# Zeros below the upper activations: the FFN tail's second product on 128 rows in place of 64

## The chip, the cores and the metric

The kernel runs on one core of one Trainium2 chip. The metric is the device time in microseconds (us) of one execution. A core has TensorE (PE in the profile; its weight loads stand apart as PEld), VectorE (DVE), ScalarE (ACT), GpSimd (POOL) and SyncE (SP, which issues most DMAs). Each engine works through its own instructions in order; semaphores tie the engines together. A product on TensorE is two instructions: a weight load (LDWEIGHTS) of the stationary block and a MATMUL that streams the moving block past it.

## The reference, cut to what matters

The model is a trunk of two layers on 512 tokens of 1024 features in float32. Each layer has an FFN, a token mixer and a second FFN; a last RMSNorm ends it. The FFN is the part that the change touches, and it runs four times:

```python
D_FF = 2752
def swiglu(h, w_gate, w_up, w_down):
    return (jax.nn.silu(h @ w_gate) * (h @ w_up)) @ w_down
x = x + 0.5 * swiglu(rmsnorm(x, ffn1_norm[layer]), ...)
```

2752 is 21 blocks of 128 hidden features and a rest of 64. This rest is the tail.

## The kernel before, in words

Features lie on the 128 partitions (rows), tokens along the free dimension. Every float32 operand of a product is split in an upper part ("hi", a rounded copy) and a lower part ("lo", what the rounding left), and a product of two operands is three matmuls: `whi*xhi`, `wlo*xhi`, `whi*xlo` (`mm3`, L244 to L246). The weight blocks come by DMA as `raw`; ACT makes `whi` (L206) and DVE `wlo` (L212), two units ahead of the products that use them.

An FFN goes in thirds of its hidden features: 8, 7 and then 7 blocks, the last of these being the tail (block 21). For each block there is a gate unit and an up unit of 24 matmuls (`over_x`, into banks `ps_A`). VectorE and ScalarE turn their results into `hhi` and `hlo`. After each third come eight down units, one for each 128 output features (`down`, into banks `ps_mm`): three matmuls for each hidden block, then `x += 0.5*ps` (L475) and the next norm's scaled and split input (L297, L303) and squares.

The tail's gate and up parts, 64 features each, share one unit. Its evacuation is `evac_tail` (L436 to L451), which stands first in the third, some 12 units ahead of the down units. It leaves the activations in a tile `both`: the upper part on rows 0 to 63 and the lower part on rows 64 to 127. The down weights' last block holds the same 64 rows twice. So one 128-row matmul (L470) gives `whi*hhi + whi*hlo`, and a second one on rows 0 to 63 alone (L471) gives `wlo*hhi`:

```python
both = st.h[TAIL][0]
nc.tensor.matmul(ps, u.hi[:, j * 128:(j + 1) * 128], both, start=False, stop=False)
nc.tensor.matmul(ps, u.lo[0:64, j * 128:(j + 1) * 128], both[0:64], start=False, stop=True)
```

A down unit of the last third thus has 20 matmuls: 18, L470 and L471. The next unit starts with a 128-row product again. In the fourth FFN the last third's down units run in two passes, one for each half of the tokens (`last_down`, L540 and L541, 256 columns), so that the final norm can begin early; its factors are broadcast by L583 after the third unit of the second pass.

The order on every engine is the order of emission. Outside the first layer's mixer that is the order of the Python code; in the mixer a planner sets it from fixed estimates, which do not depend on the FFN. During the first FFN, DVE, POOL and PE also work out tables for the mixer between the units (L735 to L954).

Of the kernel before, what the change touches and what calls it, by code (L numbers as in the profile page):

```python
# [46 lines left out]
class Unit:  # L47
    """A stationary weight block [128, cols], the products that use it and what follows them."""

# [9 lines left out]
class Sched:  # L59
    """Orders tasks on the engines by estimated start, then priority, and emits them in that order.  # L60

    A task takes tokens (tile slots) when it starts and gives tokens back when it ends; tokens go to
    the waiting tasks in order of priority, but for the tags in `loose`. A task of `any` engine goes to
    the one of its (engine, duration) pairs that ends first, and gets it as its argument."""

# [73 lines left out]
class Trunk:  # L139
# [6 lines left out]

    # ---------------------------------------------------------------- set-up
    def pools(self):
# [41 lines left out]

    # ---------------------------------------------------------------- weight stream
    def load(self, n):
# [22 lines left out]
    def advance(self):  # L215
        """Splits the next weight block and loads one further ahead."""
        n = self.split
        if n < len(self.units):
            self.cut_hi(n)
            self.cut_lo(n)  # L220
        if n + RAW_BUFS < len(self.units):
            self.load(n + RAW_BUFS)

    def drive(self):
        """Emits the steps in order; weights are loaded and split ahead of their products."""
        self.prologue()
        for s in self.steps:
            if isinstance(s, Unit):
                if s.own is None:
                    self.advance()  # L230
                s.products(s)
                if s.after is not None:
                    s.after()
                if s.own is not None:
                    self.advance()
            else:
                s()

    def mm3(self, ps, pairs, start=True, stop=True):
        """ps += sum over (whi, wlo, xhi, xlo) of the product at float32's accuracy."""  # L240
        nc = self.nc
# [6 lines left out]
    def over_x(self, tag, keep):  # L248
        """Products of one [1024 -> 128] block with the scaled activations."""

# [11 lines left out]
    def over_x_two(self, tag, units, keeps):  # L262
        """The products of two blocks in turns, so that each part of x serves both when it comes."""
        banks = []
# [7 lines left out]

    # ---------------------------------------------------------------- norms
    def feed_norm(self, which, k):
        """Adds tile k of x to the sum of squares and makes its part of x*g, split."""
        self.feed_xg(which, k)
        self.feed_sq(which, k)
# [60 lines left out]
    def norm_mm(self):  # L338
        """Sums over the features, tokens on the partitions."""
        self.nps = self.bank("mm")  # L340
        for t in range(4):
            self.nc.tensor.matmul(
                self.nps[:, t:t + 1], self.acc[:, t * 128:(t + 1) * 128], self.ones[:, 0:1], start=True, stop=True)
# [5 lines left out]
    def norm_pow(self, n=4):  # L349
        """(mean(x^2) + eps)^-1/2."""  # L350
        self.np_ = self.tp.tile([128, 4], F32, tag="np", name="np_", bufs=2)
        self.nc.gpsimd.tensor_tensor(self.np_[:, 0:n], self.nv[:, 0:n], self.mhalf[:, 0:n], ALU.pow)

    def norm_r(self, n=4, at=0):
        """One Newton step."""
        v, p = self.nc.vector, self.np_[:, 0:n]
# [9 lines left out]
    def norm_diag(self, n=4):  # L366
        """r on the diagonal, split."""
        v = self.nc.vector
# [29 lines left out]

    # ---------------------------------------------------------------- SwiGLU
    def ffn(self, n, nxt):  # L400
        """x += 1/2 FFN n; nxt names the norm that follows."""
        st = self
# [34 lines left out]
        def evac_tail(keep):  # L437
            def run():
# [11 lines left out]
                nc.vector.tensor_tensor(both[64:128], s[64:128], hi[64:128].bitcast(F32), ALU.subtract)  # L450
                st.h[TAIL] = (both, None)  # L451
            return run

        def down(dt, third):
# [4 lines left out]
            def products(u):  # L459
# [7 lines left out]
                if TAIL in fs:  # L467
                    j = nf - 1
                    both = st.h[TAIL][0]
                    nc.tensor.matmul(ps, u.hi[:, j * 128:(j + 1) * 128], both, start=False, stop=False)  # L470
                    nc.tensor.matmul(ps, u.lo[0:64, j * 128:(j + 1) * 128], both[0:64], start=False, stop=True)  # L471

# [43 lines left out]
    def last_down(self, units):  # L516
        """The last products and the final norm, one half of the tokens after the other.

        The first half is scaled with its features on the partitions; the second is transposed while
        its norm is worked out."""  # L520
        st, nc = self, self.nc
# [7 lines left out]
        def products(dt, h):  # L529
# [8 lines left out]
            j = len(full)  # L538
            both = st.h[TAIL][0]
            nc.tensor.matmul(p, u.hi[:, j * 128:(j + 1) * 128], both[:, c], start=False, stop=False)  # L540
            nc.tensor.matmul(p, u.lo[0:64, j * 128:(j + 1) * 128], both[0:64, c], start=False, stop=True)  # L541

# [17 lines left out]
        def sums(h, n):  # L560
            """The squares of all features but the last 128, then of these."""
            if n == 0:
# [69 lines left out]

    # ---------------------------------------------------------------- gated short convolution
    def short_conv(self, nxt):
# [71 lines left out]

    # ---------------------------------------------------------------- S5 tables
    def bc(self, ap, shape, axis):
        return ap.unsqueeze(axis).to_broadcast(shape)

    def exp_poly(self, out, x, tmp, itmp):
        """exp of a small tile in float32 by range reduction and a polynomial."""
        nc = self.nc
# [19 lines left out]
    def cmul_parts(self, v, orr, oi, ar, ai, br, bi, t):  # L733
        """(orr + i oi) = (ar + i ai)(br + i bi); the results may not overlay the operands."""
        v.tensor_tensor(orr, ar, br, ALU.mult)  # L735
# [11 lines left out]
    def s5_tables(self):  # L747
        """Works out the S5 tables and leaves them in DRAM by quarter (8 groups), in small pieces."""
        st, nc, a = self, self.nc, self.a
# [208 lines left out]

    # ---------------------------------------------------------------- layer 0: S5 beside stick-breaking attention
    def masks(self):  # L960
        """-[k' >= k], -1, the causal mask's -1e30 and the identity, for float32r products."""
        nc = self.nc
# [21 lines left out]
    def mixer(self, nxt):  # L984
        """Layer 0's token mixer as tasks of the engines."""
        st, nc, a = self, self.nc, self.a
# [29 lines left out]

        # ---- weights
        units = []

        def stream(src, prio):  # L1020
            """A further weight block; its task ends when it is loaded and split."""
            u = Unit(src, 1024, None, None)
            units.append((u, prio))
            return u

        # ---- the units over x
        def over_x(src, prio, tag, gate=None):
# [25 lines left out]

        # ---- v, tokens on the partitions
        vb, vps = [], []
# [37 lines left out]

        # ---- S5
        tab_t, u_t, y_t, h_t = {}, {}, {}, {}
# [118 lines left out]

        # ---- q and k
        qk_t = {}
# [27 lines left out]

        # ---- attention
        c_t, w_t, s_t, scored, split = {}, {}, {}, {}, {}
        ORDER = (1, 3, 2, 0)

        def head(h):
# [99 lines left out]
            def values():  # L1349
                """Rows 0 to 63 gather the products of v's upper part, rows 64 to 127 those of its lower part."""  # L1350
                o = H["o"] = st.bank("mm")
# [34 lines left out]

        # ---- the S5 gate
        add(None, 0, None, [qus[7].last] + [u.last for u in qus], 130.0, rel=["xhi"] * 8 + ["xlo"] * 8)
# [26 lines left out]
        def quarter(u, j, src, deps, prio, rel):  # L1415
            """Products of the j-th [512 -> 128] block of a unit with four split tiles."""
            X = {}
# [56 lines left out]

        # ---- the output projection, S5's half and attention's
        x_t = {}
# [23 lines left out]

        # ---- the weight stream
        units.sort(key=lambda x: x[1])
# [23 lines left out]

    # ---------------------------------------------------------------- ends
    def prologue(self):
# [37 lines left out]
    def warm_up(self):  # L1566
        """Keeps the tensor engine busy, so that its clock is up when the first data comes."""
        t = self.bank("mm")
# [68 lines left out]
def layout(i):  # L1637
    """The inputs as the device reads them: blocks that are contiguous on each partition."""
    import numpy as np
# [60 lines left out]
def result(got):  # L1700
    """The tokens' first half lies with features first, the second with tokens first."""
    import numpy as np
# [18 lines left out]
```

## Time and profile before

| what | value |
| --- | --- |
| median of 3 runs (lowest, highest) | 1892.98 us (1892.46, 1894.23) |
| profiled execution, first to last instruction | 1893.3 us |
| PE busy | 1878.5 us, 99% |
| PEld busy | 1539.3 us, 81% |
| DVE, ACT, POOL busy | 1052.8, 611.2, 130.3 us |
| mean granted TensorE clock | 0.996 of full |

The profiled execution's own time is its span of 1893.3 us; the page gives nothing that lies outside it. The median of the runs is 0.3 us less. Matmuls are pipelined and the profile models their ends, so that a duration (0.39 us) overlaps the next one; what a product costs is read from the distance between two starts.

### The profile page before, as it was taken

What the parts mean: (1) busy time and instruction counts of PE and PEld (TensorE: products, weight loads), DVE (VectorE), ACT (ScalarE), POOL (GpSimd) and SP (SyncE); (2) the same over time, 40 slices, a digit from 0 to 9 for tenths busy, and PEclk for the clock granted to TensorE, in tenths of its full rate; (3) what the DMA queues carried; (4) which work ended last, traced back from release to release, by engine and by line L of the source; (5) the groups of instructions that cost most, each with busy time, mean ns of one, the idle gap of its engine ahead of it and who ended that gap; (6) DMA issues with size and microseconds to landing.
All of it is one profiled execution on the core that took longest, in us unless ns stands there. A gap on an engine that the chain in (4) does not pass through costs nothing.

```text
span 1893.3 us, 21863 instructions
## 1 busy us (share of the span) xinstructions
PE 1878.5 (99%) x8562; PEld 1539.3 (81%) x8562; DVE 1052.8 (56%) x1617; ACT 611.2 (32%) x854; POOL 130.3 (7%) x247
## 2 busy tenths in 40 slices
PE   9999999999999999999999999999999999999998
PEld 7888888788777888888878888887788888888888
DVE  6657777556898553444455434445555554344453
ACT  4312222323764432222232222233322332122233
POOL 0280000100020200000010000000100100000000
PEclk9999999999989999999999999999999999999999
DMA  4334344446211232222222322322222223223231
GB/s 156 118 95 145 111 146 128 130 161 217 79 45 54 72 112 98 100 89 101 94 96 96 96 98 92 98 100 89 101 98 92 95 90 105 100 89 96 96 107 47
DMA packets 76551, 195.63 MB, mean 103 GB/s; under 512 B 20048, under 2 KB 27232, under 8 KB 76448
## 3 DMA queue, kind: packets, MB, share of 16 engines
q1 hardware_dynamic: 76272, 194.20, 31.3%
q8 instruction: 67, 1.10, 0.2%
q14 instruction: 36, 0.29, 0.0%
q10 hardware_dynamic: 144, 0.03, 0.0%
q0 software_dynamic: 32, 0.01, 0.0%
HBM read 180.45 MB, written 12.58 MB: 102 GB/s over the span
## 4 chain that ended last, share of the span: by engine, by line
PE 95%; DVE 2%; DMA 1%; ACT 1%; issue 0%; SPq 0%; POOL 0%; DVEq 0%; POOLq 0%; ACTq 0%
PE ps_A L244 19%; PE ps_A L246 19%; PE ps_A L245 19%; PE ps_mm L244 9%; PE ps_mm L246 9%; PE ps_mm L245 9%; PE ps_A L1037 1%; PE ps_mm L1425 1%; PE ps_A L1039 1%; PE ps_A L1038 1%; PE ps_mm L1426 1%; PE ps_mm L1427 1%; PE ps_A L1323 1%; PE ps_mm L471 1%; PE ps_A L1269 1%
## 5 line engine op out<-in xcount | busy, mean ns | idle before, releaser
L244 PE MATMUL ps_A<-xhi,whi 128*128 128x512 f32 x1568 | 612.9, 391 | 0.8 <-ACT whi L1557 0.8
L245 PE MATMUL ps_A<-xhi,wlo 128*128 128x512 f32 x1568 | 611.2, 390 | 0.5 <-DVE wlo L1558 0.5
L246 PE MATMUL ps_A<-xlo,whi 128*128 128x512 f32 x1568 | 610.9, 390 | 0.0
L212 DVE TENSOR_TENSOR wlo<-raw,whi 128x1024 fp32r<-128x1024 f32 (+1 forms) x322 | 399.0, 1240 | 122.3 <-ACT whi L206 120.7
L206 ACT CAST whi<-raw 128x1024 fp32r<-128x1024 f32 (+1 forms) x324 | 331.4, 1024 | 392.7 <-PE ps_mm L246 232.5
L244 PEld LDWEIGHTS ps_A<-xhi,whi 128*128 128x128 f32 x1568 | 294.8, 188 | 63.7 <-ACT whi L1557 1.4
L245 PEld LDWEIGHTS ps_A<-xhi,wlo 128*128 128x128 f32 x1568 | 294.8, 188 | 62.6 <-DVE wlo L1558 1.1
L246 PEld LDWEIGHTS ps_A<-xlo,whi 128*128 128x128 f32 x1568 | 294.7, 188 | 61.6
L244 PE MATMUL ps_mm<-hhi,whi 128*128 128x512 f32 (+1 forms) x672 | 262.5, 391 | 0.0
L246 PE MATMUL ps_mm<-hlo,whi 128*128 128x512 f32 (+1 forms) x672 | 258.5, 385 | 0.0
L245 PE MATMUL ps_mm<-hhi,wlo 128*128 128x512 f32 (+1 forms) x672 | 257.3, 383 | 0.0
L475 DVE SCALAR_TENSOR_TENSOR x<-ps_mm,x 128x512 f32<-128x512 f32 x88 | 60.8, 691 | 170.6 <-PE ps_mm L246 152.3
L244 PEld LDWEIGHTS ps_mm<-hhi,whi 128*128 128x128 f32 x672 | 126.3, 188 | 30.5 <-issue 5.6
L246 PEld LDWEIGHTS ps_mm<-hlo,whi 128*128 128x128 f32 x672 | 126.2, 188 | 27.5
L245 PEld LDWEIGHTS ps_mm<-hhi,wlo 128*128 128x128 f32 x672 | 126.2, 188 | 25.5
L421 ACT ACTIVATE s<-t 128x512 f32<-128x512 f32 x84 | 53.1, 632 | 290.4 <-DVE t L419 290.4
L432 ACT CAST hhi<-s 128x512 fp32r<-128x512 f32 x84 | 52.2, 621 | 288.7 <-DVE s L431 288.7
L419 DVE TENSOR_TENSOR t<-ps_A,rb 128x512 f32<-128x512 f32 x84 | 57.9, 690 | 110.6 <-PE ps_A L246 104.4
L431 DVE TENSOR_TENSOR s<-ps_A,s 128x512 f32<-128x512 f32 x84 | 58.0, 690 | 108.0 <-PE ps_A L246 107.4
L422 DVE TENSOR_TENSOR s<-s,rb 128x512 f32<-128x512 f32 x84 | 58.3, 694 | 63.3 <-ACT s L421 63.3
L293 POOL TENSOR_TENSOR acc<-acc,sq 128x512 f32<-128x512 f32 x28 | 36.4, 1300 | 827.9 <-issue 623.1
L433 DVE TENSOR_TENSOR hlo<-s,hhi 128x512 fp32r<-128x512 f32 x84 | 58.2, 693 | 57.7 <-ACT hhi L432 57.7
(350 smaller groups left out, 1607.0 us busy)
## 6 DMA issues: line engine op xcount, KB each, us to landing
raw<-gu SPq DMA_DIRECT2D x170, 512.0 KB, 3.3
raw<-dn SPq DMA_DIRECT2D x64, 448.0 KB, 3.3
raw<-dn SPq DMA_DIRECT2D x32, 512.0 KB, 3.5
raw<-sci SPq DMA_DIRECT2D x24, 512.0 KB, 3.2
raw<-ab SPq DMA_DIRECT2D x16, 512.0 KB, 3.3
raw<-abo SPq DMA_DIRECT2D x8, 512.0 KB, 3.3
raw<-sco SPq DMA_DIRECT2D x8, 512.0 KB, 3.2
x<-xT SPq DMA_DIRECT2D x8, 256.0 KB, 5.4
```

What stands on the lines that cost most here:

```text
L206: self.nc.scalar.copy(u.hi[:, : u.cols], u.raw[:, : u.cols])
L212: (engine or self.nc.vector).tensor_tensor(u.lo[:, :c], u.raw[:, :c], u.hi[:, :c].bitcast(F32), ALU.subtract)
L244: nc.tensor.matmul(ps, whi, xhi, start=start and i == 0, stop=False)
L245: nc.tensor.matmul(ps, wlo, xhi, start=False, stop=False)
L246: nc.tensor.matmul(ps, whi, xlo, start=False, stop=stop and i == n - 1)
L419: nc.vector.tensor_tensor(t, pg, st.rb, ALU.mult)
L421: nc.scalar.activation(s, t, AF.Silu)
L422: nc.vector.tensor_tensor(s, s, st.rb, ALU.mult)
L431: nc.vector.tensor_tensor(s, pu, s, ALU.mult)
L432: nc.scalar.copy(hi, s)
L433: nc.vector.tensor_tensor(lo, s, hi.bitcast(F32), ALU.subtract)
L475: nc.vector.scalar_tensor_tensor(x, keep[0], 0.5, x, ALU.mult, ALU.add)
```

## The change

The tail's upper part gets a tile of its own, `hi`, on all 128 rows: the activations on rows 0 to 63 (a third ScalarE copy) and zeros on rows 64 to 127 (a memset on GpSimd, once DVE has read what stood there). The second product then runs on all 128 rows of the lower weights, with this tile as its moving operand. The rest of the diff takes out comments; from L451 on, lines stand two lower in the changed kernel.

```diff
 evac_tail:
                 nc.scalar.copy(hi[64:128], s[64:128])
                 nc.scalar.copy(both[0:64], s[64:128])
                 nc.vector.tensor_tensor(both[64:128], s[64:128], hi[64:128].bitcast(F32), ALU.subtract)
-                st.h[TAIL] = (both, None)
+                nc.scalar.copy(hi[0:64], s[64:128])
+                nc.gpsimd.memset(hi[64:128].bitcast(F32), 0.0)
+                st.h[TAIL] = (both, hi)
 down:
-                    both = st.h[TAIL][0]
+                    both, upper = st.h[TAIL]
                     nc.tensor.matmul(ps, u.hi[:, j * 128:(j + 1) * 128], both, start=False, stop=False)
-                    nc.tensor.matmul(ps, u.lo[0:64, j * 128:(j + 1) * 128], both[0:64], start=False, stop=True)
+                    nc.tensor.matmul(ps, u.lo[:, j * 128:(j + 1) * 128], upper, start=False, stop=True)
 last_down:
-            both = st.h[TAIL][0]
+            both, upper = st.h[TAIL]
             nc.tensor.matmul(p, u.hi[:, j * 128:(j + 1) * 128], both[:, c], start=False, stop=False)
-            nc.tensor.matmul(p, u.lo[0:64, j * 128:(j + 1) * 128], both[0:64, c], start=False, stop=True)
+            nc.tensor.matmul(p, u.lo[:, j * 128:(j + 1) * 128], upper[:, c], start=False, stop=True)
```

On PE no instruction is added or moved. This is the end of a down unit of the first FFN's last third and the start of the next, before and then after (`hi_2427` is the new tile).

```order
L246 MATMUL ps_mm<-hlo,whi 128x512
L470 MATMUL ps_mm<-both,whi 128x512
L471 MATMUL ps_mm<-both,wlo 128x512
L244 MATMUL ps_mm<-hhi,whi 128x512
L245 MATMUL ps_mm<-hhi,wlo 128x512
```

```order
L246 MATMUL ps_mm<-hlo,whi 128x512
L472 MATMUL ps_mm<-both,whi 128x512
L473 MATMUL ps_mm<-hi_2427,wlo 128x512
L244 MATMUL ps_mm<-hhi,whi 128x512
L245 MATMUL ps_mm<-hhi,wlo 128x512
```

The second product keeps its place and takes another moving tile. (The shape in these rows is that of the result.)

On POOL the memset comes in among the table memsets of the first FFN. The first fence is before, the second after; `np_` is the norm's power, `acc` the sum of squares.

```order
L906 MEMSET qco 128x8
L907 MEMSET qsi 128x8
L906 MEMSET qco 128x8
L907 MEMSET qsi 128x8
L293 TENSOR_TENSOR acc<-acc,sq 128x512 x7
```

```order
L908 MEMSET qco 128x8
L909 MEMSET qsi 128x8
L452 MEMSET hi_2427 64x512
L908 MEMSET qco 128x8
L909 MEMSET qsi 128x8
L293 TENSOR_TENSOR acc<-acc,sq 128x512 x7
```

The zeros stand behind the third pair of table memsets and ahead of the fourth. In each of the other three FFNs the memset stands between the norm's power and the next work of POOL. On ACT the third copy stands right behind the second one, once for each FFN.

## Rows read from the trace of the kernel before

**Rows 1.** The profile page: busy time, share and instructions of each engine.

```profile
PE 1878.5 (99%) x8562; PEld 1539.3 (81%) x8562; DVE 1052.8 (56%) x1617; ACT 611.2 (32%) x854; POOL 130.3 (7%) x247
```

**Rows 2.** The profile page: shares of the chain of waits that ended last.

```profile
PE 95%; DVE 2%; DMA 1%; ACT 1%; issue 0%; SPq 0%; POOL 0%; DVEq 0%; POOLq 0%; ACTq 0%
```

**Rows 3.** Timeline of FFN 1's first tail: start, duration, engine, line, shapes, [idle before].

```profile
347.25 0.39 PE L245 MATMUL ps_mm<-hhi,wlo 128*128 128x512 f32 x1
...
348.87 0.39 PE L246 MATMUL ps_mm<-hlo,whi 128*128 128x512 f32 x1
348.87 0.19 PEld L470 LDWEIGHTS ps_mm<-both,whi 128*128 128x128 f32 x1
349.10 0.39 PE L470 MATMUL ps_mm<-both,whi 128*128 128x512 f32 x1
349.42 0.18 PEld L471 LDWEIGHTS ps_mm<-both,wlo 64*128 64x128 f32 x1 [0.36 <-issue]
...
349.85 0.19 PEld L244 LDWEIGHTS ps_mm<-hhi,whi 128*128 128x128 f32 x1 [0.25 <-issue]
...
350.19 0.39 PE L245 MATMUL ps_mm<-hhi,wlo 128*128 128x512 f32 x1
...
350.42 0.40 PE L246 MATMUL ps_mm<-hlo,whi 128*128 128x512 f32 x1
```

**Rows 4.** Chain of waits in order of time, second FFN: first and last tail.

```profile
949.54 0.43 PE ps_mm L471
...
984.53 0.43 PE ps_mm L471
```

**Rows 5.** Timeline of the fourth FFN's first pass, around its second tail.

```profile
1841.50 0.28 PE L244 MATMUL ps_A<-hhi,whi 128*128 128x256 f32 x1
...
1842.10 0.29 PE L246 MATMUL ps_A<-hlo,whi 128*128 128x256 f32 x1
...
1843.07 0.28 PE L246 MATMUL ps_A<-hlo,whi 128*128 128x256 f32 x1
```

**Rows 6.** Waits of the weight loads: us in total, times, longest.

```profile
PEld ps_mm L471 <- issue: 8.6, 24, 0.4
PEld ps_mm L244 <- issue: 5.6, 23, 0.2
```

**Rows 7.** Line 541, the tail's second product in the fourth FFN: durations, first and last start.

```profile
L541 PE MATMUL ps_A<-both,wlo x8: 379/379/379, 1839.7 to 1859.1; 64*128 64x256 f32 x8
...
L541 PE MATMUL ps_mm<-both,wlo x8: 379/379/379, 1861.8 to 1882.4; 64*128 64x256 f32 x8
```

**Rows 8.** Groups by line: two weight loads of attention | busy, mean ns | idle before.

```profile
L1270 PEld LDWEIGHTS ps_A<-qkhi,qklo 64*128 64x128 f32 x32 | 6.1, 191 | 0.0
...
L1269 PEld LDWEIGHTS ps_A<-qkhi 64*128 64x128 f32 x32 | 6.0, 186 | 4.8 <-issue 3.7
```

**Rows 9.** Line 449, the second ScalarE copy: ns min/median/max, first and last start.

```profile
L449 ACT CAST both<-s x4: 618/618/619, 275.2 to 1775.3; 64x512 fp32r<-64x512 f32 x4
```

**Rows 10.** Line 906, the table memsets on POOL, the same columns.

```profile
L906 POOL MEMSET qco<- x4: 112/112/113, 139.5 to 291.4; 128x8 f32 x4
```

**Rows 11.** Groups by line on POOL: the largest memset | busy, mean ns | idle.

```profile
L774 POOL MEMSET mtab<- 128x1024 f32 x1 | 1.0, 961 | 0.1
```

**Rows 12.** Windows: PE, PEld, DVE, ACT, POOL busy, PE clock, DMA share, GB/s.

```profile
945.00:985.00 40.00, 40.00 (x162) 29.38 (x161) 22.87 (x25) 16.23 (x23) 7.80 (x6) 1.00 0.29 95
386.00:640.00 254.00, 247.51 (x1235) 201.41 (x1234) 185.27 (x345) 131.79 (x229) 30.34 (x22) 0.98 0.33 110
```

**Rows 13.** Timeline of the second pass, around L583.

```profile
1867.91 0.48 DVE L376 TENSOR_SCALAR diag<-ident,nl 128x128 fp32r<-128x128 f32 x2
...
1868.29 0.38 PE L541 MATMUL ps_mm<-both,wlo 64*128 64x256 f32 x1
...
1868.60 0.38 PE L583 MATMUL ps_A<-diag,onesr 128*128 128x256 f32 x1
```

## The prediction

> **What bounds the kernel now.** I read the page first. TensorE is busy for 99% of the span, no other engine for more than 56% [rows 1], and the chain that ended last runs over PE for 95% of it [rows 2]. So the time is, but for some waits in the mixer and at the ends, the sum of the distances between the starts of successive matmuls, and a change on another engine counts only where PE comes to wait for it. The question is then what the distances are around the tail.
>
> The timeline of the first tail answers it [rows 3]. From L245 at 347.25 to L246 at 348.87 lie seven ordinary steps: 1.62 / 7 = 0.231 us each. The reader is to see how that pace is kept: the load for L470 starts at 348.87, together with the matmul ahead of it, so it is done when its own matmul can start. L470 itself, on 128 rows and with `both` as its moving tile, starts one ordinary step later (348.87 to 349.10). Then the pattern breaks. The 64-row load of L471 doesn't start beside L470; it starts at 349.42, 0.32 us after L470, and the weight loads stood idle for 0.36 us before it with nothing that the profile could name ("issue"). It breaks a second time on the way back: the 128-row load of the next unit's L244 starts at 349.85, again after 0.25 us of unnamed idle time, 0.43 us behind L471; the step after that, to L245 at 350.19, is 0.34 us. From 350.19 to 350.42 the ordinary pace is back.
>
> That it is the change of rows and not 64 rows as such is to be seen in attention. There three 64-row products follow each other. The first one's load, which comes behind a 128-row product, collects 4.8 us of idle time over 32 of them, 3.7 of it unnamed; the second one's load, of the same shape, collects 0.0 [rows 8].
>
> **The change part by part.** *The 512-column tails.* From L246 at 348.87 to L246 at 350.42 are five steps, 1.55 us; five ordinary ones are 5 x 0.231 = 1.16. The tail thus costs 0.39 us over the ordinary pace. The second FFN gives it again by another way: its first and last L471 lie 34.99 us apart, seven units of 20 products, 5.00 us a unit [rows 4]; less 20 x 0.231 = 4.63 that leaves 0.37. I take 0.39, which is measured within one tail, and keep 0.37 for the range. There are 24 such tails [rows 6], eight in each of three FFNs: 24 x 0.39 = 9.4 us.
>
> *The 256-column tails.* In the fourth FFN five ordinary steps take 1842.10 - 1841.50 = 0.60 us, 0.12 each; the five steps over the tail, from L246 at 1842.10 to L246 at 1843.07, take 0.97 [rows 5]. Excess 0.37 us, nearly what it is at 512 columns, so it doesn't scale with the columns. There are 8 + 8 of them [rows 7]: 16 x 0.37 = 5.9 us.
>
> After the change, the second product has 128 rows like both its neighbours, so neither load meets another shape. No row shows this product with the new tile. Its nearest row is L470, the same shape over the same weights' block, at an ordinary step [rows 3]; that is the value I take, and the whole excess goes. From below, it can't come under the ordinary step, since it streams as many columns as the others. From above, it would keep the step that L471 has today (0.32 in place of 0.23), for a reason of its own such as its new tile: then 40 x 0.09 = 3.6 us stay.
>
> *The third ScalarE copy.* Four of them at 0.62 us, as the second copy takes [rows 9]. They stand on ACT in the unit of the tail, ahead of the next weight block's upper split. That split is made two units ahead of its products, some 10 us, and ACT is busy for a third of the time [rows 1]. Cost: nothing. Without that cover it would be 4 x 0.6 = 2.5 us.
>
> *The memset.* The only one on wide tiles is 0.96 us for 1024 columns [rows 11]; 512 columns would by that be an estimated 0.5 us, four times. In the first FFN it stands on POOL behind the third pair of table memsets and ahead of the fourth, and the fourth started at 291.4 us [rows 10]. The first product that reads the zeros comes at 349.42, so there are 58 us to spare; in the other FFNs POOL has nothing queued ahead of it but a norm's work that is long done. Queued behind it are small table memsets and sums of squares, and PE waits for none of them within those 58 us. Cost: nothing.
>
> *What is late next.* A down unit shrinks from 5.0 to 4.6 us. Over eight units, VectorE is busy for 22.9 of 40 us, ScalarE for 16.2, POOL for 7.8, and the DMA engines for 29% [rows 12]: 2.9 us a unit at most, far below 4.6. One place is tight. In the second pass of the fourth FFN, L583 starts at 1868.60, and the diagonal it multiplies was ready at 1867.91 + 0.48 = 1868.39, a margin of 0.21 us [rows 13]. That DVE chain hangs on the tail of the unit before, and the PE time between the two shrinks by one tail, 0.37. So L583 will wait for about 0.37 - 0.21 = 0.16 us, a new wait, once; I charge 0.2.
>
> **Sum.** 9.4 + 5.9 - 0.2 = 15.1 us off the profiled execution: 1893.3 - 15.1 = 1878.2. The median of the runs lay 0.3 below that execution: 1877.9 us.
>
> **The rivals.** *The mixer swallows the first FFN's share.* The first FFN's 8 x 0.39 = 3.1 us are given back if something that the FFN doesn't pace, such as the tables that go out to DRAM during it, then holds the mixer. For it: between 386 and 640 us PE isn't full (247.5 of 254 us busy) and its clock isn't either (0.98) [rows 12], so PE there does wait for others. Against it: the work it waits for starts from the FFN's results, and DVE, busy for 185 of these 254 us, gets its input earlier too. Time: 1877.9 + 3.1 = 1881.0.
>
> *It does nothing.* The unnamed idle time would belong to the end of an accumulation group or to the last block's weights, and padding rows would leave it. Time: 1893.0, the median as it is. Against it: of the 96 down units 64 have no tail, and their first loads stand behind a closed group as well; but in all only 23 loads of L244 into `ps_mm` waited so, 5.6 us in all or 0.24 each, as after the tail in the timeline [rows 3, 6]. And L470 reads that same block of the weights at full pace. This is also what a rule of the Trainium skill would make of the change: "TensorE: Matmul & The Clock Gate", under "Why this matters for your kernels", says that a single matmul over 32 rows takes as long as one over 128, which taken by itself makes the padding free and worthless, a sum of 0. The same page, under "The mechanism", lets a weight load overlap a running matmul only where the two lie in different row groups; by that a full-row load couldn't start beside a full-row product at all. The trace doesn't agree with that one: L470's load does just that at 348.87 [rows 3].
>
> *Slower, by late zeros.* Now the second product also waits for POOL's memset and ACT's copy, where before it waited for a copy alone. If POOL in the first FFN were held at the fourth pair's place by its DMA, PE would stand at its first tail, at 349 us. Each us of delay past that is a us lost; the change turns slower by over 0.2% when it exceeds 15.1 + 3.8 = 18.9 us, with the zeros written only at 368 us. Time at that point: 1896.8. Against it: the memset stands ahead of the fourth pair, and that itself ran at 291.4 [rows 10].
>
> **How the numbers follow.** The forecast has 84 in 100, the mixer's share lost 9, no effect 5, slower 2. What a measurement of this kernel can tell from no change is about 0.2%, 3.8 us; the first two lie beyond that on the fast side: faster 0.93, same 0.05, slower 0.02. The range: from above, the step of 0.32 gives 1877.9 + 3.6 = 1881.5, and the mixer's rival 1881.0; with half a us for the runs' spread, 1882. From below, an excess of 0.43 in place of 0.39 (if ordinary steps are a hundredth of their length shorter elsewhere, 20 x 0.002 = 0.04 by the way of rows 4) adds 24 x 0.04 = 1.0 us, no wait at L583 0.2, and the lowest run lay 0.5 below the median: 1876.2; I go down to 1875.5, since the two readings of the excess (0.39 and 0.37) already differ by 0.02 a tail, 0.8 us over 40.
>
> **What would show it.** In the changed kernel's timeline the load of L473 starts together with the matmul of L472, without idle time, and steps around the tail are 0.23 us (0.12 in the fourth FFN). The unnamed waits of L471 and of L244 behind it are gone from the list of waits; successive tails of the second FFN lie 4.6 us apart. L583 shows a short wait for the diagonal. The memset starts near 276 us. I am wrong if the load of L473 still starts 0.3 us behind L472 (no effect), or if the tails get closer but the mixer's stretch from its first product to its last grows by some 3 us.

## The result and the profile after

The changed kernel took 1877.67 us (median of 4 runs, 1876.42 to 1880.74); the kernel before, with one run more, 1893.61 (median of 4, 1892.46 to 1906.06). Run against run the ratio is 0.991, 95% interval 0.9887 to 0.9933: 0.9% faster. The forecast was 1877.9. A second set of 5 runs gave 1877.12 and 0.9911 (0.9896 to 0.9926).

The page after, to be held against [rows 1, 2]: TensorE is as full as it was, it only has 17 us less to do, and the chain still runs over it for 95%.

```profile
PE 1861.5 (99%) x8562; PEld 1538.6 (82%) x8562; DVE 1052.5 (56%) x1617; ACT 613.1 (33%) x858; POOL 132.4 (7%) x251
...
PE 95%; DVE 2%; issue 1%; ACT 1%; DMA 0%; POOL 0%; SPq 0%; DVEq 0%; POOLq 0%; ACTq 0%
```

The timeline of the first tail after (start, duration, engine, line, operands), against [rows 3]:

```profile
347.15 0.39 PE L246 MATMUL ps_mm<-hlo,whi 128*128 128x512 f32 x1
347.15 0.19 PEld L472 LDWEIGHTS ps_mm<-both,whi 128*128 128x128 f32 x1
347.38 0.40 PE L472 MATMUL ps_mm<-both,whi 128*128 128x512 f32 x1
347.38 0.19 PEld L473 LDWEIGHTS ps_mm<-hi,wlo 128*128 128x128 f32 x1
347.61 0.40 PE L473 MATMUL ps_mm<-hi,wlo 128*128 128x512 f32 x1
347.61 0.19 PEld L244 LDWEIGHTS ps_mm<-hhi,whi 128*128 128x128 f32 x1
347.85 0.40 PE L244 MATMUL ps_mm<-hhi,whi 128*128 128x512 f32 x1
...
348.08 0.39 PE L245 MATMUL ps_mm<-hhi,wlo 128*128 128x512 f32 x1
...
348.31 0.39 PE L246 MATMUL ps_mm<-hlo,whi 128*128 128x512 f32 x1
```

Each load now starts with the matmul ahead of it, and both idle times are gone. From L246 to L246 the five steps take 1.16 us where they took 1.55. The chain of waits gives the second FFN's first and last tail, against [rows 4]:

```profile
943.77 0.23 PE ps_mm L473
...
975.82 0.23 PE ps_mm L473
```

That is 32.05 / 7 = 4.58 us a unit, after 5.00. In the list of the weight loads' waits L473 no longer stands, and of the 23 unnamed waits of L244 [rows 6] two are left:

```profile
PEld ps_mm L244 <- issue: 0.4, 2, 0.2
```

Line 543, the second product in the fourth FFN (durations in ns, first and last start), against [rows 7]:

```profile
L543 PE MATMUL ps_A<-hi,wlo x8: 278/279/282, 1827.1 to 1843.9; 128*128 128x256 f32 x8
...
L543 PE MATMUL ps_mm<-hi,wlo x8: 281/284/289, 1846.3 to 1864.5; 128*128 128x256 f32 x8
```

Seven units of the first pass take 16.8 us in place of 19.4, of the second 18.2 in place of 20.6.

**Where the profiled 18.2 us came from.** By the starts of the tails in both traces, a unit went from 5.04 to 4.65 us in the first FFN and from 5.00 to 4.58 in the second and third: 8 x 0.40 + 16 x 0.42 = 9.9 us. From the fourth FFN's first tail to the end it was 1893.3 - 1839.7 = 53.6 and is 1875.1 - 1827.1 = 48.0: 5.6 us. Together 15.5. The other 2.7 us are not the change's. Some 1.7 of them are gone within the first 30 us, long before the first tail. The windows (PE, PEld, DVE, ACT, POOL busy, then the granted clock) show why; first the kernel before, then the one after:

```profile
0.00:30.00 30.00, 27.68 (x115) 22.66 (x116) 18.66 (x30) 17.82 (x25) 3.26 (x14) 0.94 0.59 211
```

```profile
0.00:30.00 30.00, 28.18 (x122) 23.11 (x123) 20.39 (x38) 17.85 (x25) 3.25 (x14) 1.00 0.62 212
```

The profiled execution of before spent part of this stretch at 1.2 GHz (a mean of 0.94), and the one after didn't. It isn't the change that decides this: two executions of one program below show 0.94 and 1.00. The last 0.9 us lie in the mixer, whose length wanders: from the first FFN's last tail to the second FFN's first it took 564.7 us before (0.4 of them that last tail's own), 563.5 after, and 567.5 in the profile of the second set, of the same kernel as after.

### The profile page after: what moved, and what is told of

Same layout as the page of the kernel before. It is cut to its first block, busy times and chain, and to the rows that moved or that the text cites. A ratio compares the mean times of both kernels' runs of the same rounds, so it can differ in the third digit from the quotient of the medians.

```text
span 1875.1 us, 21874 instructions
## 1 busy us (share of the span) xinstructions
PE 1861.5 (99%) x8562; PEld 1538.6 (82%) x8562; DVE 1052.5 (56%) x1617; ACT 613.1 (33%) x858; POOL 132.4 (7%) x251
## 4 chain that ended last, share of the span: by engine, by line
PE 95%; DVE 2%; issue 1%; ACT 1%; DMA 0%; POOL 0%; SPq 0%; DVEq 0%; POOLq 0%; ACTq 0%
PE ps_A L244 19%; PE ps_A L245 19%; PE ps_A L246 19%; PE ps_mm L244 9%; PE ps_mm L246 9%; PE ps_mm L245 8%; PE ps_A L1039 1%; PE ps_A L1041 1%; PE ps_A L1040 1%; PE ps_mm L1427 1%; PE ps_mm L1428 1%; PE ps_mm L1429 1%; PE ps_A L1325 1%; PE ps_A L1271 0%; PE ps_mm L940 0%
## 5 line engine op out<-in xcount | busy, mean ns | idle before, releaser
L244 PE MATMUL ps_A<-xhi,whi 128*128 128x512 f32 x1568 | 612.1, 390 | 0.5 <-ACT whi L1559 0.5
L246 PE MATMUL ps_A<-xlo,whi 128*128 128x512 f32 x1568 | 610.6, 389 | 0.0
L244 PEld LDWEIGHTS ps_A<-xhi,whi 128*128 128x128 f32 x1568 | 294.5, 188 | 62.9 <-ACT whi L1559 1.3
L246 PEld LDWEIGHTS ps_A<-xlo,whi 128*128 128x128 f32 x1568 | 294.5, 188 | 61.9
L244 PE MATMUL ps_mm<-hhi,whi 128*128 128x512 f32 (+1 forms) x672 | 259.6, 386 | 0.0
L246 PE MATMUL ps_mm<-hlo,whi 128*128 128x512 f32 (+1 forms) x672 | 258.5, 385 | 0.0
L246 PEld LDWEIGHTS ps_mm<-hlo,whi 128*128 128x128 f32 x672 | 126.2, 188 | 27.4
L244 PEld LDWEIGHTS ps_mm<-hhi,whi 128*128 128x128 f32 x672 | 126.4, 188 | 25.3 <-issue 0.4
L297 ACT ACTIVATE xhi<-x,norms 128x512 fp32r<-128x512 f32 x48 | 34.6, 724 | 103.1 <-DVE x L477 62.5
```

The costliest lines, as they stand in the source:

```text
L244: nc.tensor.matmul(ps, whi, xhi, start=start and i == 0, stop=False)
L246: nc.tensor.matmul(ps, whi, xlo, start=False, stop=stop and i == n - 1)
```

## The experiments

The theory: TensorE pays at each change of the number of rows between neighbouring products, some 0.20 us at each of the tail's two changes, and the padded product takes both away. The first rival was that something else of the tail costs: the end of the group, the 64-row product itself, or the tile. Intervals are of the ratio to the kernel before.

**64 rows again, with the new tile.** The copy and the memset stay.

```diff
-nc.tensor.matmul(ps, u.lo[:, j * 128:(j + 1) * 128], upper, start=False, stop=True)
+nc.tensor.matmul(ps, u.lo[0:64, j * 128:(j + 1) * 128], upper[0:64], start=False, stop=True)
```
(and the same in `last_down`)

> The changed kernel with its second tail product back on rows 0 to 63 of the new tile; the third ScalarE copy and the memset stay. Theory (each change of the number of rows between neighbouring products costs, about 0.2 us an edge, two edges a tail): all of the gain goes, 1893 us, and the second FFN's down units lie 5.0 us apart again. Rival (the new tile or its place is what helped, not the rows): as the changed kernel, 1877.7. Rival (copy and memset cost something): slower than 1893 by up to 4.5 us.

Measured: 1893.21 us, 0.9995 (0.9979 to 1.0012). The waits are back as they were:

```profile
PEld ps_mm L473 <- issue: 8.7, 24, 0.4
PEld ps_mm L244 <- issue: 5.6, 23, 0.2
```

The second FFN's units are 5.00 us apart again. So the whole gain hangs on the rows; the tile, the copy and the memset neither give nor take anything that this measurement, good to some 3 us either way, can tell.

**128 rows in three FFNs only.** The line in `last_down` alone is as before.

> 128 rows in the first three FFNs, 64 rows in the two passes of the fourth. Theory: the price is per tail and nearly the same at 512 and 256 columns; the 24 tails of the first three FFNs give 9.9 us (3.1 + 3.4 + 3.4 by the two traces), so about 1883 to 1884; units of the fourth FFN stay 2.77 us apart. Rival (the price goes with the columns, so most of it is in the 512-column tails): below 1880.

Measured: 1884.72, 0.9947 (0.993 to 0.9964), 8.3 us below the 1893.03 beside it and a little above the expected 1883 to 1884. The interval holds the expected 9.9 us, but the time alone doesn't part theory and rival. The 512-column tails stream three quarters of the tails' columns, so a price by the column would give 0.75 x 15.5 = 11.6 us, a ratio of 0.9939, and the interval holds that too; the rival's 1880 was set too low. The trace does part them. It has 4.58 us a unit in the second and third FFN, and in the fourth's first pass (line 543, first and last start)

```profile
L543 PE MATMUL ps_A<-hi,wlo x8: 381/382/384, 1830.5 to 1849.9; 64*128 64x256 f32 x8
```

which is 19.4 / 7 = 2.77 us a unit, against 16.8 / 7 = 2.40 in the changed kernel. A half-wide tail thus costs 0.37 us, nearly as much as one twice as wide (0.40 to 0.42): the price goes by the tail, not by the column.

**The 64-row product second in its unit**, so that a 128-row product ends the group.

```diff
+nc.tensor.matmul(ps, u.hi[:, j * 128:(j + 1) * 128], both, start=True, stop=False)
+nc.tensor.matmul(ps, u.lo[0:64, j * 128:(j + 1) * 128], both[0:64], start=False, stop=False)
 st.mm3(ps, [...], start=False)
```
(shortened; the two lines at the unit's end go, and the same in `last_down`)

> The kernel before, with the tail's two products put first in their unit: L470's product opens the group, the 64-row product comes second, the 18 others follow, so that the group ends with a 128-row product. Theory: both changes of rows remain, no gain: 1893, units 5.0 us apart. Rival (the price belongs to the end of a group, where the 64-row product stood): as the changed kernel, 1877.7, units 4.6 us apart.

Measured: 1892.88, 0.9992 (0.9977 to 1.0008): no gain. The idle times went with the product into the middle of the group (timeline, second FFN):

```profile
954.17 0.40 PE L466 MATMUL ps_mm<-both,whi 128*128 128x512 f32 x1
...
954.50 0.18 PEld L467 LDWEIGHTS ps_mm<-both,wlo 64*128 64x128 f32 x1 [0.36 <-issue]
...
954.93 0.19 PEld L244 LDWEIGHTS ps_mm<-hhi,whi 128*128 128x128 f32 x1 [0.25 <-issue]
...
955.27 0.39 PE L245 MATMUL ps_mm<-hhi,wlo 128*128 128x512 f32 x1
```

The rival of the group's end is out.

**64-row products in pairs.** In even units the product stays last, in odd ones it comes first.

```diff
+if dt % 2 and TAIL in fs:
+    nc.tensor.matmul(ps, u.lo[0:64, ...], both[0:64], start=True, stop=False)
+    nc.tensor.matmul(ps, u.hi[:, ...], both, start=False, stop=False)
+    st.mm3(ps, [...], start=False)
+else:
     # as before
```
(shortened; the same in `last_down`)

> The kernel before, with the 64-row product last in even units and first in odd ones, so that two of them are neighbours. Theory (price per change of rows): of four changes in a pair of units two go; 12 pairs at 512 columns (0.41 each), 4 in the fourth FFN's first pass and 2 in its second (0.37 each; the other two pairs there have sums or the broadcast between them) give 7.1 us: about 1886. Rival (price per 64-row product, wherever it stands): 1893.

Measured: 1885.83, 0.9954 (0.9938 to 0.997): 7.2 us below the 1893.03 beside it, 7.1 expected, with as many 64-row products as before. One pair's timeline takes the price apart:

```profile
945.35 0.40 PE L481 MATMUL ps_mm<-both,whi 128*128 128x512 f32 x1
...
945.67 0.49 PE L482 MATMUL ps_mm<-both,wlo 64*128 64x512 f32 x1
945.78 0.19 PEld L467 LDWEIGHTS ps_mm<-both,wlo 64*128 64x128 f32 x1
946.01 0.39 PE L467 MATMUL ps_mm<-both,wlo 64*128 64x512 f32 x1
...
946.33 0.50 PE L468 MATMUL ps_mm<-both,whi 128*128 128x512 f32 x1
...
946.67 0.39 PE L244 MATMUL ps_mm<-hhi,whi 128*128 128x512 f32 x1
946.67 0.19 PEld L245 LDWEIGHTS ps_mm<-hhi,wlo 128*128 128x128 f32 x1
946.90 0.40 PE L245 MATMUL ps_mm<-hhi,wlo 128*128 128x512 f32 x1
```

The load of L467, 64 rows behind 64 rows, starts 0.23 us ahead of its matmul, as any other does. Each change makes two steps longer: the one into it (0.32 from L481, 0.32 from L467) and the one behind it (0.34 each), against 0.23: 0.09 + 0.11 = 0.20 us a change. The tail's own steps of 0.32, 0.43 and 0.34 [rows 3] are two such changes one product apart.

**No zeros at all.** The kernel before, with the second product on 128 rows of `both`. It adds the product of the two lower parts where the changed kernel adds zeros.

```diff
-nc.tensor.matmul(ps, u.lo[0:64, j * 128:(j + 1) * 128], both[0:64], start=False, stop=True)
+nc.tensor.matmul(ps, u.lo[:, j * 128:(j + 1) * 128], both, start=False, stop=True)
```
(and the same in `last_down`)

> The kernel before, with the second tail product on all 128 rows of the lower weights and the tile that the first product streams (both), without the new tile, the third copy and the memset: it adds the product of the two lower parts, where the changed kernel adds zeros. Theory (only the number of rows counts; copy and memset are hidden): the time of the changed kernel within 0.1%, 1877 to 1878. Rival (zeros on half of the rows do something themselves): more, up to 1893.

Measured: 1877.37, 0.9912 (0.9896 to 0.9928), and the changed kernel beside it:

> The changed kernel again, beside the three others of this set. Theory: 15.5 us less than before by the two traces (3.1 + 3.4 + 3.4 in the first three FFNs, 5.7 in the fourth), a ratio of 0.9918; 1877 to 1878.

1877.12, 0.9911 (0.9896 to 0.9926). The same time without the third copy, the memset and the longer use of a tile. The run without zeros is also one that shows the start's clock of 0.94, with its first tail at 349.6 us; when the same program ran again (the last experiment), the clock there was 1.00 and the first tail came at 347.6:

```profile
0.00:30.00 30.00, 27.21 (x113) 22.37 (x114) 18.29 (x28) 17.75 (x25) 3.19 (x14) 0.94 0.64 211
```

```profile
0.00:30.00 30.00, 27.75 (x122) 22.93 (x123) 20.35 (x38) 17.84 (x25) 3.26 (x14) 1.00 0.61 212
```

**Attention's changes, by new tasks.** Each of the 32 score blocks is a 128-row mask product and three 64-row ones [rows 8], and pays the same price. This is one of them, with 512 columns, in the changed kernel (TensorE alone):

```profile
498.31 0.22 PE L1270 MATMUL ps_A<-mk_mask,mk_eye 128*128 128x128 f32 x1
498.46 0.49 PE L1271 MATMUL ps_A<-qkhi 64*128 64x512 f32 x1
498.80 0.39 PE L1272 MATMUL ps_A<-qkhi,qklo 64*128 64x512 f32 x1
499.03 0.39 PE L1273 MATMUL ps_A<-qklo,qkhi 64*128 64x512 f32 x1
499.35 0.50 PE L1039 MATMUL ps_A<-xhi,whi 128*128 128x512 f32 x1
499.69 0.40 PE L1040 MATMUL ps_A<-xhi,wlo 128*128 128x512 f32 x1
```

L1272, a 64-row product with 64-row products on both sides, takes the ordinary 0.23 us; the steps at the two changes are 0.34 behind the first, 0.32 into the second and 0.34 behind it.

Two versions brought the 64-row products together by merging the planner's tasks: two by two on top of the change, then four by four on top of the version without zeros.

```diff
-for i in ORDER:
-    last = sm[i] = urg("PE", pe(128) + 3 * pe(w), score(i), deps, p, acq=[] if i == 3 else ["A"])
+for two in (ORDER[0:2], ORDER[2:4]):
+    last = urg("PE", cost, score(two), deps, p, acq=["A"] if 3 in two else ["A", "A"])
```
(shortened; `score` is changed to match)

> The changed kernel, with attention's score tasks taken two by two: the two 128-row mask products first, then the six 64-row products, so that 16 of 32 pairs of changes of rows go. Theory (same price, about 0.40 us a pair, where PE bounds the mixer): 6.4 us of PE time, of which half or more shows, since PE is idle for only 6.5 of the mixer's 254 us: 1871 to 1874.5. Rival (the mixer hangs on VectorE and ScalarE, which now get their first scores later): 1877 or more.

> As the run with the tile both in the second product, and with the four score tasks of a head in one: four mask products, then twelve 64-row products; 24 of 32 pairs of changes go, 9.6 us of PE time. Theory: 1868 to 1873 if PE bounds the mixer. Rival (the planner needs three banks at once, and the mask and score work of a head holds up what stood between): no gain over 1877, or a loss of some us.

Measured: 1891.43, 0.9984 (0.9967 to 1.0), and 1884.23, 0.9945 (0.993 to 0.9959): 14 and 7 us slower than the changed kernel. Both times are the rivals'. The windows of the mixer, first of the changed kernel, then of the one with tasks two by two:

```profile
380.00:640.00 260.00, 254.23 (x1269) 207.23 (x1268) 186.88 (x350) 132.72 (x230) 31.34 (x23) 0.98 0.34 110
```

```profile
380.00:640.00 260.00, 242.32 (x1210) 198.95 (x1209) 185.26 (x345) 130.80 (x230) 27.21 (x20) 0.97 0.33 104
```

PE stands for 17.7 of 260 us where it stood for 5.8, at a lower mean clock. The two largest of its waits (us in total, times, longest) are for attention's results from DVE and ACT:

```profile
PE ps_mm L1435 <- DVE os L1377: 5.7, 3, 4.7
PE ps_A L1270 <- ACT w L1338: 3.6, 1, 3.6
```

In the changed kernel these two were 2.1 and 1.4 us. Whether the planner's new order did this or the later scores as such, these two runs don't tell.

**Attention's changes, with the plan as it was.** Now a head's fourth score block is emitted at the second's place, in the bank that they share anyway, and the planner still plans two tasks. Without the zeros in the tail.

```diff
+if i == 3:
+    return
+mine = (1, 3) if i == 1 else (i,)
+for n in mine:
+    nc.tensor.matmul(H["z", n][:, 0:128], st.eye, st.mask, start=n != 3, ...)
+for n in mine:
+    part(n, qhi, qlo, khi, klo)
```
(shortened; `part` holds the three 64-row products)

> The run with the tile both in the second product, and in each of eight heads the products of the fourth score block put right behind those of the second, at the second's place, while the planner still plans them as two tasks: VectorE, ScalarE, POOL and SyncE keep their order word for word. Theory (each pair of changes of rows costs 0.40 us on PE, and what the pairwise and fourfold score tasks lost came from the planner's new order): 8 pairs go, 3.2 us of PE time at most, 1 to 3 us of it in the total: 1874 to 1876.5. Rival (the scores' early products themselves hold up what VectorE waits for): 1878 or more, with PE waiting longer in the mixer.

> The run with the tile both in the second product once more, on the same chip as the run beside it: 1877 to 1878, 15.5 us less than before.

Measured: 1876.33, 0.9915 (0.9899 to 0.9931), beside 1878.43, 0.992 (0.9906 to 0.9934), which is 14.0 us less than before where 15.5 were expected; the interval holds both. The changes went: unnamed waits of the first score product fell from 18 (3.6 us) to

```profile
PEld ps_A L1274 <- issue: 2.0, 10, 0.3
```

and the time didn't rise. But 2.1 us between the medians lie within the intervals, and the profiled mixers differ by 2.7 us where two of one kernel differ by 4. That it is faster is not shown. What it does show is that early scores alone, eight of them, cost nothing that the measurement could tell. That leaves the planner's new order, or the later and larger blocks that came with it, as the likelier cause of the two losses; neither was tried by itself, so the cause stays open.

## Why the prediction was right

**What bounds the kernel.** That the time is the sum of the distances between matmul starts, and that a change on another engine counts only where PE waits for it, held: the distances around the tails account for 15.5 us, the medians for 15.9, and 64 rows again, with the copy and the memset kept, gave the old time.

**512-column tails.** 9.4 us were forecast, 9.9 measured. The term was a little too small, by the ordinary step that it was reckoned with: 0.39 us was read in the first FFN, where a step takes 0.231 us and the change gave 0.40. In the second and third FFN an ordinary step is 4.58 / 20 = 0.229, so the unit of 5.00 us held 0.42. The reading of [rows 4] with the first FFN's step came out too low (0.37) for that reason.

**256-column tails, and the late diagonal.** 5.9 - 0.2 = 5.7 forecast, 5.6 measured. The new wait is there, and it is the only new one among the fourth FFN's down units:

```profile
1851.86 0.48 DVE L376 TENSOR_SCALAR diag<-ident,nl 128x128 fp32r<-128x128 f32 x2
1851.96 0.28 PE L543 MATMUL ps_mm<-hi,wlo 128*128 128x256 f32 x1
...
1852.08 0.70 PE L585 MATMUL ps_A<-diag,onesr 128*128 128x256 f32 x2
...
1852.39 0.19 PEld L585 LDWEIGHTS ps_A<-diag,onesr 128*128 128x128 f32 x1 [0.20 <-DVE diag L376]
1852.50 0.19 PEld L244 LDWEIGHTS ps_mm<-hhi,whi 128*128 128x128 f32 x1
1852.61 0.28 PE L244 MATMUL ps_mm<-hhi,whi 128*128 128x256 f32 x1
```

From L543 to the next unit's L244 lie 0.65 us; three ordinary steps would be 0.36. So 0.29 us were lost there, where 0.16 were reckoned and 0.2 charged. The reckoning took the start of L583's first product (1868.60) as what has to wait. In this trace it is the second of the two that waits, at its weight load: by the ordinary pace this load would start with the first product, at 1852.08, but the diagonal's lower part was ready only at 1851.86 + 0.48 = 1852.34.

**Copy and memset.** Hidden, as said (the version without them took 1877.37 beside 1877.12), and of the size that was said (ns min/median/max, first and last start):

```profile
L451 ACT CAST hi<-s x4: 612/612/614, 274.0 to 1763.3; 64x512 fp32r<-64x512 f32 x4
```

```profile
L452 POOL MEMSET hi<- x4: 521/522/522, 274.4 to 1763.6; 64x512 f32 x4
```

The zeros were there 73 us before the first product that reads them (347.6). The estimate from the wide memset [rows 11] was 0.5 us.

**The rivals.** "It does nothing" (1893.0) fell with the time itself; the run with the middle position took its first reason, the end of the group, the version without zeros its second, the last block's weights, which it reads on all rows at the ordinary pace, and the pairs showed that a 64-row product as such isn't dear. With it fell, as a guide to the sum of this kernel, the Trainium skill's rule in "TensorE: Matmul & The Clock Gate" ("Why this matters for your kernels"), that a single matmul over 32 rows takes as long as one over 128. The rule holds of the product, here at 64 rows: L1272 in attention takes the ordinary 0.23 us. It doesn't hold of the steps beside a change of rows, which cost 0.20 us a change. Another page of the Trainium skill, "TensorEngine Tiling (Array Packing)" ("Key Properties"), says that changing the tiling mode drains TensorE. The pair's timeline fits that and gives a price, 0.20 us; that the tail's change of rows is such a change of mode, no run here shows.

That the mixer would swallow the first FFN's share is not borne out. The rival's 1881.0 is a ratio of 0.9937, above the intervals of both sets (up to 0.9933 and 0.9926). The sign that the prediction named for it, a mixer's stretch some 3 us longer, did appear in one profile of the changed kernel (567.5 us against 564.7, from the first FFN's last tail to the second's first), so one trace wouldn't have settled it. In the four others with a 128-row tail in the first FFN and the mixer as it was, the stretch took 563.5, 565.2, 563.2 and 564.9 us; in three with the 64-row tail 564.7, 563.4 and 564.2, with 0.4 of each the last tail's own. The means differ by 1.1 us, less than two executions of one kernel do, so a loss of that size is neither shown nor ruled out. Late zeros were never near.

**The sum.** 15.1 forecast, 15.5 by the traces, 15.9 and 16.3 between the medians of the changed kernel's two sets. That the first median, 1877.67, came so near to 1877.9 is in part luck, for its four runs lie between 1876.42 and 1880.74. And the 0.3 us by which the median was said to lie below the profiled execution set a run's time against a span: a run's time is 1.7 to 2.1 us longer than its own span (1876.82 and 1875.1 for the profiled run after), so the profiled execution of before was some 2 us slower than the median. The forecast doesn't suffer from it, since it comes to taking 15.1 us off the median of before.

## What to carry to other kernels

Where TensorE is full, read the distances between starts and look for unnamed idle time of the weight loads: here a 64-row product between 128-row ones was no cheaper by itself and made three steps longer (0.32, 0.43 and 0.34 us in place of 0.23). So pad such a product (with zeros, or with rows that already lie there and do no harm), or put such products next to each other. Count the changes, not the columns: 40 narrow products of 8562 held 0.8% of this kernel. Where a planner sets the order, try first to change what a task emits and keep the tasks: both versions with new tasks lost more than the changes saved.

## What the runs showed of the hardware that was not expected

The price of a change of rows comes in two parts, 0.09 us on the step into it and 0.11 on the step behind it, and is about as large at 256 columns (0.37 us for two changes) as at 512 (0.39 to 0.42). Attention's score blocks show it at their own widths (0.34 in place of 0.23 us behind the change at 512 columns).

Not every change of shape has this price. Attention's value products go from 128 to 64 stationary columns, on 128 rows, and back at the ordinary pace:

```profile
500.90 0.39 PE L1358 MATMUL ps_mm<-wh,v 128*128 128x512 f32 x1
501.13 0.39 PE L1359 MATMUL ps_mm<-wl,v 128*64 128x512 f32 x1
501.36 0.39 PE L1039 MATMUL ps_A<-xhi,whi 128*128 128x512 f32 x1
```

A change to 16 stationary columns, in the tables of the first FFN, has the unnamed wait and the step of 0.32 us again:

```profile
158.99 0.39 PE L246 MATMUL ps_A<-xlo,whi 128*128 128x512 f32 x1
159.31 0.22 PEld L940 LDWEIGHTS ps_mm<-qca,qb 128*16 128x16 f32 x3 [0.35 <-issue]
```

Two executions of one program, the version without zeros, came to the first tail at 349.6 and at 347.6 us; the former had part of its first 30 us at 1.2 GHz (mean clock 0.94 against 1.00). The mixer's stretch differed by 4 us between two executions of the changed kernel.
